# The second half of an out-product, its row norms and the MLP's first splits, moved into a table of ordered pieces

## The chip, the cores and the metric

One core of one Trainium2 chip. The time is device microseconds from launch to end; a run's profiled execution also gives a span, the time from its first to its last recorded instruction. TensorE, VectorE, ScalarE and GpSimd stand in the rows as PE, DVE, ACT and POOL, the queue that issues most of the loads as SP.

## The reference, cut to what matters

One encoder layer on x of 1024 tokens by 1024 features, float32. An mLSTM group (4 heads) and a differential attention group (4 heads) each give 512 features. Then:

```python
mixed = jnp.concatenate([mix_a, mix_b], axis=-1).astype(dt)
x = x + (mixed @ w_out[l]).astype(dt)
u = rms(x, norm2_g[l]).astype(dt) @ w_ff1[l]
u = jnp.square(jax.nn.relu(u))
x = x + (u @ w_ff2[l]).astype(dt)
```

`rms` divides each token by the root of the mean of its squares and multiplies by a gain. The change touches the line with `w_out`, the norm behind it and the preparation of `w_ff1`.

## The kernel before, in words

All activations lie transposed, 128 features on the partitions and tokens along the row, in two halves of 512 tokens. Every float32 product is made of three reduced-precision ones: each operand is split into a high part (ACT copies it into a rounded type) and a low part (DVE or POOL subtracts the high part from the raw value), and `mm3` issues high by high, high by low and low by high, each a matmul of 128x128 weights on a 128x512 tile. A split of a 128x1024 weight tile thus takes a load on SP into a raw buffer, a copy on ACT, a subtraction on DVE or POOL, and only then the low part's matmul can run.

**Attention.** 32 items (half, head, block of 128 queries). One item is: logits on PE and DVE, two exponentials on ACT, a weighted difference on DVE, transposes across on PE, copies on DVE and ACT, the product with the values on PE (`att_product`, line 981), a square on ACT with two small POOL operations (`att_square`, 988), a power on POOL (`att_root`, 996, through `rsqrt`, line 88), and the scaling `att_unit` on DVE (999). After every fourth item `att_turn`, `att_hi` and `att_lo` transpose the four blocks and split them into `mix`, the operand of the out-product.

**The table.** From line 1089 the order of each engine is written out by hand (`manual_schedule`): `when(t, f)` puts a piece on a heap with a due time in units of one attention item, the dictionary `A` holds the offsets, and the heap is emptied in order of time. Due times are no times on the chip: they fix only the order of the instructions on each engine and queue, and each instruction then waits for what it needs. The table holds the attention, the mLSTM group's output gates, and the out-product of the first half (`first_half`, line 1185, and `out_tile`, 1193): per output tile n = 0..7 two PE pieces of 12 matmuls, an addition of x on DVE, a square on ACT with a store, and a running sum of squares on DVE. Its weight splits come from `split_ahead` (1099), low part on POOL.

**Behind the table.** At line 1256 the hand-written order ends, and up to line 1359 the framework's planner orders the instructions by its own priorities: `load_mix(1)` (four loads of `mix` on POOL's queue), `out_product(1, ...)` (line 1029) with its splits through `split` (lines 131 to 134), the last `att_turn`, `att_hi` and `att_lo` (items 28 to 31), `row_norms(0)` (1074: eight small matmuls into `pr2`, an addition `rc` on DVE, the power on POOL, eight matmuls into `pb2`, a copy to `r2` on DVE), the normalisation of the first half (`normed`, 1325, two DVE instructions a call), its splits x1 and x2 (`cut`, 1298), and the first four splits of `w_ff1` (`w_a` with `raw_e`). In `out_product`, tile 0 and tile 1 begin before the last attention head is turned, with seven of eight feature blocks in the order (4, 5, 6, 0, 1, 2, 3, 7), and block 7 is added afterwards. The planner may place an instruction earlier than the program does, also between pieces of the table, or later.

**Behind that** the MLP has a hand-written order of its own (lines 1359 to 1787): twelve matmuls a step, `row_norms(1)` at its steps 0.95 and 1.95, then normalisation, sums and splits of the second half on DVE.

Of the kernel before, what the change touches and what calls it, by code (L numbers as in the profile page):

```python
# [16 lines left out]
P = 128  # L17
# [5 lines left out]
HB = 512  # L23
# [25 lines left out]
def hybrid_block_kernel(ctx: ExitStack, tc: tile.TileContext, xT, w_v, w_kg, w_c, w_va, w_qa, w_o, w_1, w_2, vec, rel, onehot, outT):  # L49
# [38 lines left out]
    def rsqrt(out, x, n):  # L88
        return nc.gpsimd.tensor_tensor(out, x, mhalf[:, 0:n], op=ALU.pow)
# [913 lines left out]
    def att_turn(items, V):  # L1003

        h, half = items[0].h, items[0].half
        po = psB.tile([P, HB], F32, tag="pav", name=f"pt{half}{h}")
        for it in items:
            nc.tensor.transpose(po[:, it.qi * P : (it.qi + 1) * P], it.on, ident)
        V["pr"] = po.rearrange("p (b t) -> p b t", t=P)[:, :, ::-1]

    def att_hi(it, V):
        V["mv"] = mv = mix[it.half][NH + it.h].rearrange("p i (b t) -> p i b t", t=P)
        nc.scalar.activation(mv[:, 0], V["pr"], AF.Copy, scale=dg[:, it.h : it.h + 1])
# [8 lines left out]
    def load_mix(half):  # L1022
        for h in range(NH):
            mix[half][h] = opool.tile([P, 2, HB], F32R, tag=f"mix{h}", name=f"mix{half}{h}")
            nc.gpsimd.dma_start(mix[half][h], mx_dram[h][half])

    r2, acc, rooted = {}, {}, {}

    def out_product(half, psum):
        sl = slice(half * HB, (half + 1) * HB)  # L1030
        acc[half] = opool.tile([P, HB], F32, tag="yacc", name=f"yacc{half}")
        order = (4, 5, 6, 0, 1, 2, 3, 7)
        ps, ws = {}, {}

        def load(n):
            if n < KT:
                ws[n] = split(opool, w_o[n], "wo", opool, 3, 2, nc.vector, f"wo{half}{n}")

        def part(n, first, end):
            if first == 0:  # L1040
                load(n)
                ps[n] = psum(n)
            (whi, wlo), p = ws[n], ps[n]
            for j in range(first, end):
                k = order[j]
                kt = slice(k * P, (k + 1) * P)
                mm3(p, whi[:, kt], wlo[:, kt], mix[half][k][:, 0], mix[half][k][:, 1], j == 0, j == KT - 1)


        part(0, 0, KT - 1)  # L1050
        part(1, 0, KT // 2)
        yield
        part(1, KT // 2, KT - 1)
        for n in range(KT):
            if n < 2:
                part(n, KT - 1, KT)
            else:
                part(n, 0, KT // 2)
                yield
                part(n, KT // 2, KT)  # L1060
            p = ps[n]
            yt = y[half][n]
            nc.sync.dma_start(yt, xT[n][:, sl])
            nc.vector.tensor_tensor(yt, p, yt, op=ALU.add)
            if n == 0:
                nc.scalar.activation(acc[half], yt, AF.Square)
            else:
                sq = opool.tile([P, HB], F32, tag="ysq", name=f"ysq{half}{n}", bufs=1)
                nc.scalar.activation(sq, yt, AF.Square)
                nc.vector.tensor_tensor(acc[half], acc[half], sq, op=ALU.add)  # L1070
            nc.scalar.dma_start(y_dram[half][n], yt)
            yield

    def row_norms(half):
        pc = psF.tile([P, HB], F32, tag="q2", name=f"pr2{half}")
        for t in range(4):
            nc.tensor.matmul(pc[:, t : t + 1], acc[half][:, t * P : (t + 1) * P], ones[:, 0:1], start=True, stop=True)
        rc = mpool2.tile([P, 4], F32, tag="rc", name=f"rc2{half}")
        nc.vector.tensor_scalar(rc, pc[:, 0:4], D * EPS, None, op0=ALU.add)
        rooted[half] = rsqrt(rc, rc, 4).ins  # L1080
        yield
        p = psF.tile([P, HB], F32, tag="q3", name=f"pb2{half}")
        for t in range(4):
            nc.tensor.matmul(p[:, t * P : (t + 1) * P], rc[:, t : t + 1].to_broadcast([P, P]), ident, start=True, stop=True)
        r2[half] = mpool2.tile([P, HB], F32, tag=("v", "w")[half], name=f"r2{half}")
        nc.vector.tensor_copy(r2[half], p)
# [3 lines left out]
    order.enter_context(tc.manual_schedule(engines={E.PE, E.DVE, E.Activation, E.Pool, E.SP}))  # L1090
    A = dict(
        G0=-0.05, G1=0.219, E0=0.984, E1=1.396, W=1.626, A0=2.667, A1=2.819, C0=2.714, C1=2.824, P=3.534, SQ=3.666,
        RS=3.676, ON=3.783, TU=4.131, TH=4.141, TL=4.151, LD=-2.901, LV=-1.095, PF=-4, PS=1.015, PE=0.388, PT=1.671,
        PB=1.957, PW=-3.566, PH=-2.613, PL=-1.973, PX=-0.258, SW=15.195, OF=18.423, OS=0.979, OE=0.323, OQ=0.587,
        OA=1.385, OW=-3.888, OH=-2.551, OL=-2.267,
    )
    clock[0] = -99.0

    def split_ahead(tiles, src, lo_eng, t, pre):

        T = {}

        def room():
            T[0] = tiles()
            nc.sync.dma_start(T[0][2][:, 0:1024], src)

        def hi():
            act(T[0][0][:, 0:1024], T[0][2][:, 0:1024], AF.Copy)

        def lo():  # L1110
            h, l, raw = T[0]
            lo_eng.tensor_tensor(l[:, 0:1024], raw[:, 0:1024], h[:, 0:1024].bitcast(F32), op=ALU.subtract)

        floor = A["SW"] + 0.01 if pre == "O" else -99.0
        when(max(t + A[pre + "W"], floor), room)
        when(max(t + A[pre + "H"], floor), hi)
        when(max(t + A[pre + "L"], floor), lo)
        return T
# [61 lines left out]
    def w_out(n):  # L1180
        raw = opool.tile([P, 1024], F32, tag="raw", name=f"raw_wo0{n}", bufs=2)
        hi = opool.tile([P, 1024], F32R, tag="woh", name=f"hi_wo0{n}", bufs=3)
        return hi, opool.tile([P, 1024], F32R, tag="wol", name=f"lo_wo0{n}", bufs=3), raw

    def first_half():

# [37 lines left out]
    def item_pieces(n, it):  # L1224
        def on(name, f, *args):
            when(n + A[name], f, it, *args)

        if n % 4 == 0:
            when(n + A["LD"] if n else -98.0, att_load, it)
            when(n + A["LV"] if n else -97.0, att_load_v, it)  # L1230
        for m in range(2):
            on(f"G{m}", att_logits, m)
            on(f"E{m}", att_exp, m)
            on(f"A{m}", att_across, m)
            on(f"C{m}", att_copy, m)
        on("W", att_weights)
        on("P", att_product)
        on("SQ", att_square)
        on("RS", att_root)
        on("ON", att_unit)  # L1240
        if n % 4 == 3 and n < 31:
            V = {}
            when(n + A["TU"], att_turn, items[n - 3 : n + 1], V)
            when(n + A["TH"], att_hi, it, V)
            when(n + A["TL"], att_lo, it, V)
# [3 lines left out]
    first_half()  # L1249
    for n, it in enumerate(items):  # L1250
        item_pieces(n, it)
    last = {}
    while table:
        t, _, f, args = heapq.heappop(table)
        f(*args)
    order.close()
    load_mix(1)

    def psum1(n):
        if n < 2:  # L1260
            return psB.tile([P, HB], F32, tag=("pw", "pa")[n], name=f"pw1{n}", bufs=n + 1)
        return psF.tile([P, HB], F32, tag=f"q{4 + n % 4}", name=f"pw1{n}")

    work = out_product(1, psum1)
    next(work)
    att_turn(items[28:32], last)
    att_hi(items[31], last)
    att_lo(items[31], last)
    bctx.close()


# [53 lines left out]
    def normed(l, j):  # L1325

        for n in (2 * j, 2 * j + 1):
            nc.vector.scalar_tensor_tensor(y[l][n], y[l][n], g2[:, n : n + 1], r2[l], op0=ALU.mult, op1=ALU.mult)
# [4 lines left out]
    def x_part(i, src, j):  # L1333
        return xf[i], src[j], (slice(None), slice(2 * j, 2 * j + 2))

    load_e(0)
    load_e(1)
    next(work)
    psctx.close()
    psF = ctx.enter_context(tc.tile_pool(reuse_waits="tile", name="psF", bufs=1, space=PSUM))  # L1340
    norms = row_norms(0)
    next(norms)
    for n, _ in enumerate(work):
        if n == 2:
            next(norms, None)
        if 3 <= n < 7:
            j = n - 3
            normed(0, j)
            cut(*x_part(1 + j // 2, block(j // 2, 0), j % 2))
        if 6 <= n < 10:  # L1350
            with tc.issue_after(rooted[0]):
                cut(w_a(n - 6), raw_e[n - 6])
            if n < 8:
                load_e(n - 4)
    cctx.close()
    x2pool = fctx.enter_context(tc.tile_pool(reuse_waits="tile", name="x2pool", bufs=1))
    xf |= {i: parts(x2pool, f"x{i}", [P, 4, HB]) for i in (3, 6, 5, 7, 4)}
# [22 lines left out]
    def psum(c, x):  # L1380
        q = 4 * (c % 2) + x
        if x == 0 and c < N_FIRST:
            q = (0, 1, 4, 5, 6, 7)[c]
        bank[c, x] = psF.tile([P, HB], F32, tag=f"q{q}", name=f"m{c}_{x}")
        return bank[c, x]
# [479 lines left out]
```

## Time and profile before

| | |
|---|---|
| median of 3 runs | 1292.5 us (1292.22 to 1293.47) |
| the profiled execution's own time | 1292.14 us |
| its span | 1290.4 us |
| PE busy | 1257.0 us (97%) |
| DVE, ACT, POOL busy | 860.0, 603.5, 272.6 us |
| mean granted TensorE clock | 0.993 of full speed |

Start times are microseconds from the span's start. In the timeline a row gives start, duration, engine, line, operation, output<-inputs and shapes; a bracket at the end is the idle time of the engine before that row and what released it. The rows of a matmul overlap: the distance between two starts is what one costs, the duration includes its latency. The attention's last items and the first half of the out-product end near 604 us, the second half ends where the first matmul of the MLP begins, and the MLP runs to the end.

### The profile page before, as it was taken

The page shows a single profiled execution, that of the slowest core. Times are in us where ns is not written, and L with a number is a line of the kernel's source. Part 1 is how long each engine was busy: PE and PEld are TensorE (multiplying, and loading weights), DVE is VectorE, ACT ScalarE, POOL GpSimd, SP SyncE. Part 2 cuts the span into 40 slices and gives each one's busy share as a digit, 9 for nine tenths or more (in the row PEclk, how much of TensorE's full clock was granted, in tenths as well). Part 3 has the DMA queues.
Part 4 walks back from the last instruction along what each step waited for, and adds up shares of the span by engine and source line. Part 5 has one row for each costly group of instructions (what it writes and reads, how often), then busy time and mean ns, then how long its engine had stood idle before and what let it go on. Part 6 is the DMA issues. An engine that isn't in the chain of part 4 may idle for free.

```text
span 1290.4 us, 17143 instructions
## 1 busy us (share of the span) xinstructions
PE 1257.0 (97%) x6443; PEld 1038.3 (80%) x6443; DVE 860.0 (67%) x1159; ACT 603.5 (47%) x1033; POOL 272.6 (21%) x273
## 2 busy tenths in 40 slices
PE   8999999999999989999999999999999999999998
PEld 6898678887878877888777788888887888888887
DVE  8635547886338888786748887666664675458754
ACT  5323336676535565563526554454444343333332
POOL 6623312554234344332000000000000000004001
PEclk9999999999999999999989999999999999999999
DMA  6415054544165475526524574454439946344732
GB/s 201 135 54 175 24 190 108 123 123 147 72 201 195 146 263 189 177 98 214 179 95 158 188 244 163 148 163 131 154 118 330 328 163 212 116 145 148 236 114 90
DMA packets 101459, 208.32 MB, mean 161 GB/s; under 512 B 8688, under 2 KB 21744, under 8 KB 101376
## 3 DMA queue, kind: packets, MB, share of 16 engines
q1 hardware_dynamic: 78368, 154.50, 37.6%
q10 hardware_dynamic: 15008, 31.50, 6.5%
q0 software_dynamic: 8000, 21.24, 5.0%
q8 instruction: 50, 0.82, 0.3%
q14 instruction: 33, 0.27, 0.1%
HBM read 148.90 MB, written 58.29 MB: 161 GB/s over the span
## 4 chain that ended last, share of the span: by engine, by line
PE 83%; DVE 8%; DMA 3%; issue 2%; ACT 2%; POOL 1%; SPq 0%; DVEq 0%; ACTq 0%; POOLq 0%
PE z L1707 8%; PE z L1705 8%; PE z L1706 8%; PE m L1376 7%; PE m L1377 7%; PE m L1378 7%; PE pav L986 4%; PE pl L945 3%; PE pv L235 3%; PE pw L158 2%; PE pa L972 2%; PE pw L160 2%; PE pw L159 2%; PE pj_c L158 2%; PE pj_c L159 2%
## 5 line engine op out<-in xcount | busy, mean ns | idle before, releaser
L1743 POOL TENSOR_TENSOR zx<-zx,res 128x512 f32<-128x512 f32 x4 | 8.7, 2180 | 503.8 <-DVE zx L1741 503.8
L1707 PE MATMUL z<-wbh,wa0l 128*128 128x512 f32 x224 | 87.4, 390 | 0.6 <-DVE wa0l L1296 0.6
L1705 PE MATMUL z<-wbh,wa0h 128*128 128x512 f32 x224 | 87.2, 389 | 0.0
L1706 PE MATMUL z<-wbl,wa0h 128*128 128x512 f32 x224 | 87.2, 389 | 0.0
L1706 PE MATMUL z<-wel,wa1h 128*128 128x512 f32 x224 | 87.1, 389 | 0.0
L1705 PE MATMUL z<-weh,wa1h 128*128 128x512 f32 x224 | 87.1, 389 | 0.0
L1707 PE MATMUL z<-weh,wa1l 128*128 128x512 f32 x224 | 87.1, 389 | 0.0
L950 DVE CUSTOM_DVE_ANT_0 l<-pl,toe 128x1024 f32<-128x1024 f32 x64 | 76.3, 1221 | 15.5 <-PE pl L945 14.4
L956 ACT ACTIVATE l<-l,sm 128x1024 f32<-128x1024 f32 x64 | 72.9, 1141 | 1.3 <-DVE sm L950 1.3
L1296 DVE TENSOR_TENSOR wel<-g,weh 128x1024 fp32r<-128x1024 f32 x28 | 35.2, 1258 | 56.5 <-ACT weh L1293 56.5
L1425 ACT ACTIVATE sq<-sq 128x512 f32<-128x512 f32 x48 | 30.3, 632 | 90.6 <-DVE sq L1464 69.0
L1296 DVE TENSOR_TENSOR wbl<-g,wbh 128x1024 fp32r<-128x1024 f32 x28 | 35.4, 1265 | 55.9 <-ACT wbh L1293 55.9
L1293 ACT ACTIVATE weh<-g 128x1024 fp32r<-128x1024 f32 x28 | 29.7, 1060 | 90.2 <-PE z L1707 53.4
L1293 ACT ACTIVATE wbh<-g 128x1024 fp32r<-128x1024 f32 x28 | 29.7, 1061 | 89.9 <-PE z L1707 52.6
L986 PEld LDWEIGHTS pav<-v,at 128*128 128x128 f32 x512 | 62.9, 195 | 9.3 <-DVE on L1001 4.6
L986 PE MATMUL pav<-v,at 128*128 128x128 f32 x512 | 64.4, 280 | 4.5 <-DVE on L1001 2.9
L160 PE MATMUL pw<-mix,lo_wo 128*128 128x512 f32 x128 | 51.5, 402 | 4.2 <-DVE lo_wo L134 4.2
L158 PE MATMUL pj_c<-hhi,hi_c 128*128 128x512 f32 x128 | 53.5, 418 | 0.0
L945 PE MATMUL pl<-kk,q 64*128 64x512 f32 x384 | 53.3, 408 | 0.0
L158 PE MATMUL pw<-mix,hi_wo 128*128 128x512 f32 x128 | 53.2, 415 | 0.0
L159 PE MATMUL pw<-mix,hi_wo 128*128 128x512 f32 x128 | 51.1, 399 | 0.0
L159 PE MATMUL pj_c<-hlo,hi_c 128*128 128x512 f32 x128 | 50.7, 396 | 0.0
(459 smaller groups left out, 3680.2 us busy)
## 6 DMA issues: line engine op xcount, KB each, us to landing
g<-g_dram SPq DMA_DIRECT2D x56, 512.0 KB, 4.1
g_dram<-gs SPq DMA_DIRECT2D x64, 256.0 KB, 4.3
g_dram<-sq ACTq DMA_DIRECT2D x42, 256.0 KB, 2.2
kk<-k_dram POOLq DMA_DIRECT2D x16, 512.0 KB, 5.6
raw_wo<-in_w_o_dram SPq DMA_DIRECT2D x16, 512.0 KB, 4.7
re<-in_w_dram SPq DMA_DIRECT2D x16, 512.0 KB, 4.4
ro<-in_w_dram SPq DMA_DIRECT2D x16, 512.0 KB, 3.7
zt<-in_w_dram SPq DMA_DIRECT2D x16, 512.0 KB, 4.1
```

Source lines behind the costliest of these rows:

```text
L158: nc.tensor.matmul(out, ahi, bhi, start=start, stop=False)
L159: nc.tensor.matmul(out, ahi, blo, start=False, stop=False)
L160: latest[0] = nc.tensor.matmul(out, alo, bhi, start=False, stop=stop).ins
L945: nc.tensor.matmul(it.pl[x][:, sl], hd.q[r, i, qi * P : (qi + 1) * P], hd.kk[r, j, sl], start=n == 0, stop=n == 2)
L950: nc.vector.tensor_tensor_reduce(lt, it.pl[m], hd.toe[:, off : off + S], 1.0, 3.0e38, ALU.add, ALU.min, it.sm[:, m : m + 1])
L986: nc.tensor.matmul(it.pav[:, 0:P], at, it.head.v[:, c], start=c == 0, stop=c == NC - 1)
L1376: nc.tensor.matmul(p, wh, xh, start=go, stop=False, skip_group_check=True)
L1377: nc.tensor.matmul(p, wh, xl, start=False, stop=False, skip_group_check=True)
L1378: nc.tensor.matmul(p, wl, xh, start=False, stop=stop and k == 3, skip_group_check=True)
L1705: nc.tensor.matmul(p, wh, gh, start=go, stop=False, skip_group_check=True)
L1706: nc.tensor.matmul(p, wh, gl, start=False, stop=False, skip_group_check=True)
L1707: nc.tensor.matmul(p, wl, gh, start=False, stop=end, skip_group_check=True)
```

## The change

Line 1256's end of the hand-written order goes away. Everything that the planner ordered is cut into pieces with due times in the same table, the part before `bctx.close()` (due before S2 = 35.3) and the part behind it. `out_product` is deleted. `load_mix(1)` is due at 33; the PE pieces of the second half begin at 34.3 and are 0.375 apart for 12 matmuls; `split_ahead` makes its splits (high on ACT 0.861 and low on DVE 0.4 ahead of a tile's first piece, never before the tile three back has been multiplied); `row_norms(0)` comes at 36.2 and 36.9, normalisation from 37.278, the splits of `w_ff1` from 37.523. The running sum of the second half has a buffer of its own (`yacc1`). `att_lo` of all turns moves from 4.151 to 4.177.

```diff
-    r2, acc, rooted = {}, {}, {}
-
-    def out_product(half, psum):
...
+    r2, acc = {}, {}
...
-        rooted[half] = rsqrt(rc, rc, 4).ins
+        rsqrt(rc, rc, 4)
...
-        RS=3.676, ON=3.783, TU=4.131, TH=4.141, TL=4.151, LD=-2.901, LV=-1.095, PF=-4, PS=1.015, PE=0.388, PT=1.671,
+        RS=3.676, ON=3.783, TU=4.131, TH=4.141, TL=4.177, LD=-2.901, LV=-1.095, PF=-4, PS=1.015, PE=0.388, PT=1.671,
...
+        OA=1.385, OW=-3.888, OH=-2.551, OL=-2.267, HF=34.3, HS=0.375, LM=33, HE=0.3, HQ=0.415, HA=0.425, HW=-1.4,
+        HH=-0.861, HL=-0.4, HX=-3.083, S2=35.3, N0=36.2, N1=36.9, XN=37.278, XD=0.78, XH=1.108, XL=1.118, WN=37.523,
+        WD=0.8, WL=0.227, RE=35.494,
...
-        if n % 4 == 3 and n < 31:
+        if n % 4 == 3:
...
-    while table:
-        t, _, f, args = heapq.heappop(table)
-        f(*args)
-    order.close()
-    load_mix(1)
+    def h_part(V, n, first, end):
+        if first == 0:
+            V[0] = psum1(n)
+        k_order = (4, 5, 6, 0, 1, 2, 3, 7)
+        hi, lo, _ = V["w"][0]
+        for j in range(first, end):
+            k = k_order[j]
+            kt = slice(k * P, (k + 1) * P)
+            mm3(V[0], hi[:, kt], lo[:, kt], mix[1][k][:, 0], mix[1][k][:, 1], j == 0, j == KT - 1)
+
+    def h_room(n):
+        nc.sync.dma_start(y[1][n], xT[n][:, HB:])
+
+    def h_add(V, n):
+        nc.vector.tensor_tensor(y[1][n], V[0], y[1][n], op=ALU.add)
...
-    work = out_product(1, psum1)
-    next(work)
-    att_turn(items[28:32], last)
-    att_hi(items[31], last)
-    att_lo(items[31], last)
+    when(A["LM"], load_mix, 1)
+    u = A["HS"]
+    parts_at = {0: ((0, 0, 7), (3.5, 7, 8)), 1: ((1.75, 0, 4), (2.75, 4, 7), (3.75, 7, 8))}
+    ends = {0: 3.75, 1: 4.0}
+    for n in range(2, KT):
+        parts_at[n] = ((2 * n, 0, 4), (2 * n + 1, 4, 8))
+        ends[n] = 2 * n + 2.0
+    def room_at(n):
+        return A["HF"] + u * ends[n - 3] + 0.01 if n > 2 else -99.0
+
+    for n in range(KT):
+        t = A["HF"] + u * parts_at[n][0][0]
+        V = {"w": split_ahead(lambda n=n: w_out(n, 1), w_o[n], nc.vector, t, "H", room_at(n))}
+        for p, first, end in parts_at[n]:
+            when(A["HF"] + u * p, h_part, V, n, first, end)
+        t = A["HF"] + u * ends[n]
+        when(max(t + A["HX"], A["S2"] + 0.02), h_room, n)
+        when(t + A["HE"], h_add, V, n)
+        when(t + A["HQ"], h_square, V, n)
+        when(t + A["HA"], h_sum, V, n)
...
+    run(A["S2"])
     bctx.close()
...
-    load_e(0)
-    load_e(1)
-    next(work)
...
-    next(norms)
-    for n, _ in enumerate(work):
...
+    when(A["N0"], next, norms)
+    when(A["N1"], next, norms, None)
+    for j in range(4):
+        t = A["XN"] + j * A["XD"]
+        when(t, normed, 0, j)
+        when(t + A["XH"], lambda a: cut_hi(*a), x_part(1 + j // 2, block(j // 2, 0), j % 2))
+        when(t + A["XL"], lambda a: cut_lo(*a), x_part(1 + j // 2, block(j // 2, 0), j % 2))
+        t = A["WN"] + j * A["WD"]
+        when(A["RE"] if j < 2 else t - 2 * A["WD"] + A["WL"] + 0.01, load_e, j)
+        when(t, lambda c: cut_hi(w_a(c), raw_e[c]), j)
+        when(t + A["WL"], lambda c: cut_lo(w_a(c), raw_e[c]), j)
+    run(1e9)
+    order.close()
```

`split_ahead` gets a `floor` for its three due times, `w_out` takes the half, `h_square` and `h_sum` do for the second half what `square` and `sum_up` of `out_tile` do for the first.

## Rows read from the trace of the kernel before

**Rows 1.** The page: its head, and busy time by engine.
```profile
span 1290.4 us, 17143 instructions
...
PE 1257.0 (97%) x6443; PEld 1038.3 (80%) x6443; DVE 860.0 (67%) x1159; ACT 603.5 (47%) x1033; POOL 272.6 (21%) x273
```

**Rows 2.** Windows: span, busy PE, PEld, DVE, ACT, POOL, then clock, DMA share, GB/s.
```profile
640.00:650.00 10.00, 5.82 (x22) 4.42 (x21) 9.31 (x12) 4.18 (x5) 0.00 (x0) 0.82 0.09 32
```

**Rows 3.** Timeline of PE: first matmuls of stretches, and those after idle time.
```profile
297.03 0.50 PE L159 MATMUL pva<-lo_va,hhi 128*128 128x512 f32 x1 [1.61 <-POOL lo_va L603]
...
587.20 0.66 PE L1008 MATMUL pt<-ident,on 128*128 128x128 f32 x4 [0.64 <-DVE on L1001]
...
603.93 0.48 PE L158 MATMUL pw<-mix,hi_wo 128*128 128x512 f32 x1
...
604.48 0.39 PE L160 MATMUL pw<-mix,lo_wo 128*128 128x512 f32 x1
...
625.49 1.16 PE L1084 MATMUL pb<-ident,rc 128*128 128x128 f32 x8 [1.43 <-POOL rc L89]
...
647.63 0.80 PE L160 MATMUL pw<-mix,lo_wo 128*128 128x512 f32 x1 [4.18 <-DVE lo_wo L134]
648.22 0.63 PE L158 MATMUL pw<-mix,hi_wo 128*128 128x512 f32 x1
...
653.28 0.39 PE L158 MATMUL pw<-mix,hi_wo 128*128 128x512 f32 x1
...
660.79 0.39 PE L1376 MATMUL m<-x1h,wa0h 128*128 128x512 f32 x1
...
711.05 0.61 PE L1376 MATMUL m<-x4h,wd0h 128*128 128x512 f32 x1 [2.40 <-DVE sq L1464]
711.46 0.63 PE L1377 MATMUL m<-x4l,wd0h 128*128 128x512 f32 x1
```

**Rows 4.** Timeline of DVE from 578 to 665 us, the pieces that matter.
```profile
578.52 3.17 DVE L134 TENSOR_TENSOR lo_wo<-raw_wo,hi_wo 128x1024 fp32r<-128x1024 f32 x1
...
602.41 1.23 DVE L134 TENSOR_TENSOR lo_wo<-raw_wo,hi_wo 128x1024 fp32r<-128x1024 f32 x1 [0.16 <-ACT hi_wo L133]
...
604.71 0.35 DVE L1001 TENSOR_SCALAR on<-pav,sm 128x128 f32<-128x128 f32 x1 [0.25 <-POOL sm L89]
604.98 0.68 DVE L1216 TENSOR_TENSOR yacc<-yacc,ysq 128x512 f32<-128x512 f32 x1
...
640.17 2.73 DVE L1328 SCALAR_TENSOR_TENSOR y<-y,cst,r 128x512 f32<-128x512 f32 x4
...
643.96 0.69 DVE L1064 TENSOR_TENSOR y<-pw,y 128x512 f32<-128x512 f32 x1
...
646.35 2.36 DVE L134 TENSOR_TENSOR lo_wo<-raw_wo,hi_wo 128x1024 fp32r<-128x1024 f32 x2
...
664.61 0.16 DVE L1079 TENSOR_SCALAR rc<-pr 128x4 f32<-128x4 f32 x1 [1.48 <-PE pr L1077]
```

**Rows 5.** Timeline of POOL from 593 to 605 us: powers, small products, loads it issues.
```profile
593.25 1.42 POOL L89 TENSOR_TENSOR sm<-sm,mhalf 128x1 f32<-128x1 f32 x1
...
595.10 1.70 POOL L1025 DMA_DIRECT2D mix<-mx_dram  x3
598.40 0.19 POOL L994 TENSOR_TENSOR sm<-sm 128x1 f32<-128x1 f32 x1 [1.60 <-ACT on L992]
...
603.85 0.19 POOL L994 TENSOR_TENSOR sm<-sm 128x1 f32<-128x1 f32 x1 [3.46 <-ACT on L992]
604.13 0.55 POOL L89 TENSOR_TENSOR sm<-sm,mhalf 128x1 f32<-128x1 f32 x1
```

**Rows 6.** DMA: `w_out` loads 575 to 670 us, line 1025's landing, throughput 606 to 612 us.
```profile
raw_wo<-in_w_o_dram SPq DMA_DIRECT2D x7, 512.0 KB, 3.9
...
DMA to landing us min/median/max: 3.9/6.6/11.3
...
DMA packets 762, 2.09 MB, mean 349 GB/s; under 512 B 84, under 2 KB 84, under 8 KB 760
```

More of the change, by code (lines that the diff above doesn't have):

```diff
@@ L1025, in load_mix @@
             nc.gpsimd.dma_start(mix[half][h], mx_dram[h][half])
-    r2, acc, rooted = {}, {}, {}
-    def out_product(half, psum):
[L1030 to L1072, printed above, removed]
+    r2, acc = {}, {}
     def row_norms(half):
@@ L1092, in hybrid_block_kernel, with split_ahead @@
         G0=-0.05, G1=0.219, E0=0.984, E1=1.396, W=1.626, A0=2.667, A1=2.819, C0=2.714, C1=2.824, P=3.534, SQ=3.666,
-        RS=3.676, ON=3.783, TU=4.131, TH=4.141, TL=4.151, LD=-2.901, LV=-1.095, PF=-4, PS=1.015, PE=0.388, PT=1.671,
+        RS=3.676, ON=3.783, TU=4.131, TH=4.141, TL=4.177, LD=-2.901, LV=-1.095, PF=-4, PS=1.015, PE=0.388, PT=1.671,
         PB=1.957, PW=-3.566, PH=-2.613, PL=-1.973, PX=-0.258, SW=15.195, OF=18.423, OS=0.979, OE=0.323, OQ=0.587,
-        OA=1.385, OW=-3.888, OH=-2.551, OL=-2.267,
+        OA=1.385, OW=-3.888, OH=-2.551, OL=-2.267, HF=34.3, HS=0.375, LM=33, HE=0.3, HQ=0.415, HA=0.425, HW=-1.4,
+        HH=-0.861, HL=-0.4, HX=-3.083, S2=35.3, N0=36.2, N1=36.9, XN=37.278, XD=0.78, XH=1.108, XL=1.118, WN=37.523,
+        WD=0.8, WL=0.227, RE=35.494,
     )
     clock[0] = -99.0
-    def split_ahead(tiles, src, lo_eng, t, pre):
+    def split_ahead(tiles, src, lo_eng, t, pre, floor=-99.0):
         T = {}
@@ L1112, in lo @@
             lo_eng.tensor_tensor(l[:, 0:1024], raw[:, 0:1024], h[:, 0:1024].bitcast(F32), op=ALU.subtract)
-        floor = A["SW"] + 0.01 if pre == "O" else -99.0
+        floor = max(floor, A["SW"] + 0.01 if pre in "OH" else -99.0)
         when(max(t + A[pre + "W"], floor), room)
@@ L1178, in hybrid_block_kernel, with w_out @@
     ypool = yq = y = cctx = opool = None
[L1180 to L1183, printed above, removed]
+    def w_out(n, half=0):
+        raw = opool.tile([P, 1024], F32, tag="raw", name=f"raw_wo{half}{n}", bufs=2)
+        hi = opool.tile([P, 1024], F32R, tag="woh", name=f"hi_wo{half}{n}", bufs=3)
+        return hi, opool.tile([P, 1024], F32R, tag="wol", name=f"lo_wo{half}{n}", bufs=3), raw
     def first_half():
@@ L1251, in hybrid_block_kernel, with h_square, h_sum @@
         item_pieces(n, it)
-    last = {}
-    while table:
-        t, _, f, args = heapq.heappop(table)
-        f(*args)
-    order.close()
-    load_mix(1)
+    def h_part(V, n, first, end):
[11 more added lines that the diff above has]
+        nc.vector.tensor_tensor(y[1][n], V[0], y[1][n], op=ALU.add)
+    def h_square(V, n):
+        if n == 0:
+            acc[1] = opool.tile([P, HB], F32, tag="yacc1", name="yacc1")
+        V["sq"] = acc[1] if n == 0 else opool.tile([P, HB], F32, tag="ysq", name=f"ysq1{n}", bufs=1)
+        nc.scalar.activation(V["sq"], y[1][n], AF.Square)
+        nc.scalar.dma_start(y_dram[1][n], y[1][n])
+    def h_sum(V, n):
+        if n > 0:
+            nc.vector.tensor_tensor(acc[1], acc[1], V["sq"], op=ALU.add)
     def psum1(n):
@@ L1262, in psum1, with run @@
         return psF.tile([P, HB], F32, tag=f"q{4 + n % 4}", name=f"pw1{n}")
-    work = out_product(1, psum1)
-    next(work)
-    att_turn(items[28:32], last)
-    att_hi(items[31], last)
-    att_lo(items[31], last)
+    when(A["LM"], load_mix, 1)
[17 more added lines that the diff above has]
+        when(t + A["HA"], h_sum, V, n)
+    def run(until):
+        while table and table[0][0] < until:
+            _, _, f, args = heapq.heappop(table)
+            f(*args)
+    run(A["S2"])
     bctx.close()
@@ L1341, in hybrid_block_kernel @@
     norms = row_norms(0)
-    next(norms)
-    for n, _ in enumerate(work):
[L1344 to L1354, printed above, removed]
+    when(A["N0"], next, norms)
[11 more added lines that the diff above has]
+    order.close()
     cctx.close()
```

## The prediction

> **What bounds the kernel now.** The page comes first: PE is busy 97% of the span [rows 1], so a reordering can only give back PE's idle time and what its clock loses. The windows around the change come next: from 640 to 650 us PE is busy 5.82 of 10 us at a granted clock of 0.82, while DVE is busy 9.31 [rows 2]. The timeline of PE then shows each wait in the stretch that is rewritten [rows 3]. The reader is to see four things. The turn of an attention head waits 0.64 us for a scaling on DVE (587.20). The second small product of the row norms waits 1.43 us for POOL's power (625.49). A low part of tile 6's weights comes 4.18 us late (647.63). And the matmuls behind that wait run at the lower of the clock's two levels, 1.2 GHz: 12 starts from 648.22 to 653.28 take 5.06 us, where 33 starts from 653.28 to 660.79 take 7.51, or 0.228 each at 2.4 GHz. The twelve lost 5.06 - 12 x 0.228 = 2.33, and the first, 0.59 against 0.228, another 0.36: together 2.69 us.
>
> The timeline of DVE says why. The first split of the second half, which the planner placed at 578.52, took 3.17 us inside the attention, where the same shape takes 1.23 at 602.41. The splits of tiles 6 and 7 were placed at 646.35, behind normalisation (640.17) and an addition (643.96) that PE did not need yet [rows 4].
>
> **The change, part by part.** The number of matmuls, splits, additions, loads and stores stays the same; what changes is order and one more small buffer. I give times on the clock of the kernel before.
>
> 1. *The first split leaves the attention.* From 578.52, 3.17 us of DVE go, and with them the lateness that PE saw at 587.20: gain 0.64. From there to 603.93 PE had no further wait that this could shorten, so I count nothing more. Two later splits also leave; they cost PE nothing before.
>
> 2. *The first split's new place.* Its low part is now due at 33.9, behind the scaling of item 30 (33.783), and DVE's queue is in order. That scaling waits for POOL: it started at 604.71 and the next DVE instruction at 604.98 [rows 4]. The split then ends at 604.98 + 1.23 = 606.21. PE reaches tile 0 at 603.93, and the third matmul, the first with a low part, would start at 604.48 [rows 3]. New wait: 606.21 - 604.48 = 1.73 us. Queued behind it on PE are 18 more matmuls and item 31's product, and behind that its square, power, scaling and turn, all of which PE itself reaches later. The low part of tile 1 follows behind the running sum of tile 7 of the first half (0.68): 606.21 + 0.68 + 1.23 = 608.1, against 19 matmuls of tile 0 and item 31's product still to run. Hidden.
>
> 3. *Does the clock fall at that wait?* Not shown for 1.73 us. A single wait of 1.61 us (297.03) was followed by a matmul of 0.50, no half-speed run, as was the one of 1.43; the one of 2.40 at 711.05 was followed by matmuls of 0.63 [rows 3]. The bounds are 0 and 2.69 us; 1.73 lies next to 1.61, so I take 0.
>
> 4. *The four loads of `mix` on POOL's queue.* They were issued from 595.10, at 1.70 / 3 = 0.57 each; now they follow item 29's power and stand ahead of item 30's two small operations. Item 29's first operation is at 598.40; with the gaps of item 30's (603.85, 604.13, 0.55 long) its power ends at 599.23, the four issues at 601.5, 2 us before POOL is wanted at 603.85 [rows 5]. Nothing waits. Their landing took 3.9 to 11.3 us [rows 6]. PE needs the first after nine matmuls of tile 0, at 606.21 + 7 x 0.228 = 607.8; issued by 599.8, it has 8.0 us. At the median of 6.6 this costs nothing; at 11.3 from the issue's start at 599.23 it is 2.7 us late. I take 0.
>
> 5. *SP's queue.* The split of tile 2 reloads a buffer that the split of tile 0 frees, so SP stops until 606.2. Behind it stand five loads of x, two of `w_ff1` and tile 3's weights. With tile 2's own load that is 2 x 0.5 + 5 x 0.25 + 2 x 0.5 = 3.25 MiB, 9.8 us at 349 GB/s [rows 6], so tile 3 has landed by 616. It is wanted when tile 0 has got its last block and frees the high part, not before 606.21 + 43 x 0.228 = 616.0 plus item 31's product and turn. Tile 2's landing (3.9 us) is over by 610.5. The later weight loads follow a split made some 10 us before their own use. Zero; if that cover went, tile 3's split (ACT's copy and DVE's 1.23 us) would show.
>
> 6. *The row norms.* The two small products now have 12 matmuls between them, 2.7 us, for the chain DVE, POOL, PE. In the second norm the addition `rc` came at 664.61, with the MLP's first twelve matmuls just done at 660.79 + 12 x 0.228 = 663.5 as the product began, and the same spacing gave PE no wait behind it. DVE now stands still for `rc` about 4 us while PE multiplies tile 2; ahead of it is tile 3's split, so PE is not held. Gain 1.43.
>
> 7. *The later splits.* DVE's order now has the split of tile n + 2 soon behind the addition of tile n. A tile is 24 matmuls, 5.46 us. The heaviest period on DVE holds three splits, two normalisations, a sum and an addition: 3 x 1.23 + 2.73 / 2 + 0.68 + 0.69 = 6.43 us [rows 4]. There are two such periods, so additions slip by at most 1 and 2 us. Tile 6's split ends 0.69 + 2 x 1.23 = 3.15 after tile 4 does, 2.3 us before it is wanted; tile 7's ends about 1 + 0.69 + 1.23 = 2.9 after tile 5, 2.5 us before. Gain 4.18, and with the wait the 2.69 of the clock.
>
> 8. *Behind the out-product.* DVE's last piece is now one split of x2, due behind the last sum, but its high part waits on ACT behind the last square. It ends about when `rc` could start, 3.82 us after the first MLP matmul (664.61 against 660.79). Cost 0; the bounds are 0 and 1.23. The MLP's own waits (2.40 at 711.05 and smaller ones) hang on that DVE chain and move with it. Moving `att_lo` by 0.026 passes no other piece of DVE: nothing.
>
> Sum: -0.64 + 1.73 - 1.43 - 4.18 - 2.69 = -7.21 us. Against the profiled execution, 1292.14, that is 1284.9. The median of the runs is 0.36 above that execution, so I forecast **1285.3 us**. A measurement of this kernel can tell 0.2%, 2.6 us, from no change.
>
> **Rivals.**
>
> *The new wait grows.* The clock falls at the wait of point 2: 1285.3 + 2.69 = 1288.0. For it: 1.73 lies above the longest wait without a fall; against it: PE is busy without a gap for 16 us ahead. Still faster.
>
> *POOL's queue holds item 30.* A power beside a DVE instruction took 1.42 us instead of 0.55 [rows 5]. If each of the four issues is stretched by the same 0.87, they end 4 x 0.87 - 2.05 = 1.4 us too late for item 30, the wait becomes 3.1 and the clock falls: 1285.3 + 1.4 + 2.69 = 1289.4. Against it: the three issues that ran beside DVE's work at 595.10 took 0.57 each, and DVE has only short work on PSUM then. The Trainium skill, "SBUF — State Buffer", section "SBUF: two separate sides", speaks against this part of the change: VectorE and GpSimd share a port pair as an exclusive lock, and loads issued from GpSimd can be starved of descriptors while VectorE holds it. Its example, in the section "A bandwidth-pool intuition that's wrong (but worth ruling out)", stretches one such load from about 620 to 3100 ns; by that estimate four take 12.4 us, item 30 is 8.1 late, and the sum gives 1296.1, slower than before. The issues of 0.57 us beside busy DVE don't bear that out here.
>
> *DVE becomes the bound: slower.* The place is the split of tiles 6 and 7 in DVE's queue, behind splits of x1 and of `w_ff1`. If two tiles wait as tile 6 did before, each costs 4.18 + 2.69 = 6.87, and the result is 1285.3 + 13.7 = 1299.0. It decides once DVE needs more than 5.46 + 2.3 = 7.8 us for a tile's period; 6.43 is known. Splits as long as the 3.17 at 578.52 would do it, but POOL's work that stood beside that one is over by then.
>
> *Given back in the MLP.* DVE bounds PE up to 711.05. If its work there does not start earlier by what PE gains, the time stays between 1290 and 1295. Against it: `rc` starts the chain, and it follows the out-product's last sum.
>
> *The change doesn't do what it says.* Due times fix order, not time; if PE's waits hung on loads and not on order, they would stay, and so would 1292.5. The row at 647.63 names the DVE split, not a load.
>
> **Chances.** The forecast 0.55, the clock's fall at the new wait 0.18, POOL's queue by rows 0.04, no new wait at all (1283.6) 0.04; given back 0.08, no effect 0.03; DVE-bound 0.06, POOL's queue by the page's rule 0.02. Faster: 0.55 + 0.18 + 0.04 + 0.04 = 0.81. Same: 0.08 + 0.03 = 0.11. Slower: 0.06 + 0.02 = 0.08. The range goes down to no new wait and none at 711.05, 1283.6 - 2.4 = 1281.2, and up to the clock's fall with the slow landing of point 4, 1288.0 + 2.7 = 1290.7.
>
> **What would show it.** Right: no turn of a head waiting near 587; one wait of 1.5 to 2 us at the third matmul of tile 0, released by the split on DVE; full clock from there to the MLP; no wait at the second small product; the first MLP matmul near 653.6. Wrong: matmuls of 0.63 us behind the new wait, a wait on `lo_wo` at tiles 5 to 7, loads of `mix` landing after 607, or a longer distance from the first MLP matmul to the x4 wait than 711.05 - 660.79 = 50.3 us.

## The result, and the profile after

| | before | after |
|---|---|---|
| median of 4 runs each, same chip | 1292.36 us | 1286.29 us (1284.2 to 1287.63) |
| ratio, 95% interval | | 0.995 (0.9933 to 0.9968) |
| the profiled execution's own time | 1292.14 us | 1285.70 us |
| mean granted clock | 0.993 | 0.996 |

The changed kernel is 6.1 us faster by the medians, 6.4 by the profiled executions; 7.2 were forecast. The page's head and busy times, beside [rows 1]:

```profile
span 1283.9 us, 17139 instructions
...
PE 1254.5 (98%) x6443; PEld 1036.1 (81%) x6443; DVE 857.2 (67%) x1159; ACT 603.0 (47%) x1033; POOL 269.9 (21%) x273
```

The work is the same and PE's share is higher: what went is waiting. In [rows 2] PE was busy 5.82 of 10 us at a clock of 0.82. Windows of the same stretch after, with the columns of [rows 2]:

```profile
640.00:650.00 10.00, 10.00 (x46) 8.29 (x45) 10.00 (x13) 5.75 (x7) 0.00 (x0) 1.00 0.42 130
```

PE no longer pauses there, and neither does DVE: the two now run abreast. PE's timeline, beside [rows 3]:

```profile
586.00 0.66 PE L1008 MATMUL pt<-ident,on 128*128 128x128 f32 x4
...
602.74 0.48 PE L158 MATMUL pw<-mix,hi_wo 128*128 128x512 f32 x1
...
605.07 0.50 PE L160 MATMUL pw<-mix,lo_wo 128*128 128x512 f32 x1 [1.62 <-DVE lo_wo L1069]
605.40 0.40 PE L158 MATMUL pw<-mix,hi_wo 128*128 128x512 f32 x1
...
627.04 1.05 PE L1039 MATMUL pb<-ident,rc 128*128 128x128 f32 x8
...
652.45 0.39 PE L1374 MATMUL m<-x1h,wa0h 128*128 128x512 f32 x1
...
696.79 0.50 PE L1375 MATMUL m<-x7l,weh 128*128 128x512 f32 x1 [1.24 <-DVE x7l L1297]
...
703.41 0.47 PE L1374 MATMUL m<-x4h,wd0h 128*128 128x512 f32 x1 [2.40 <-DVE sq L1462]
```

The turn at 586.00 and the second small product at 627.04 have no bracket any more. The new wait, 1.62 us, stands at the third matmul of tile 0, and the matmul behind it takes 0.40: full clock. From there to the MLP PE waits for nothing. The last two rows are the MLP's, and the first of them has grown: the same matmul, 704.43 before, waited 0.54 us there.

**Where the 6.5 us of span came from.** Three stretches, each from the start of one row to that of another, and their sum:

| stretch | before | after | difference |
|---|---|---|---|
| start to the out-product's tile 0 | 603.93 | 602.74 | -1.19 |
| tile 0 to the MLP's first matmul | 56.86 | 49.71 | -7.15 |
| MLP to the end of the span | 629.6 | 631.45 | +1.84 |
| span | 1290.4 | 1283.9 | -6.5 |

The second row is the change's own, and I measure every experiment by it. Of the first, 0.64 is the turn's wait; 0.48 was there already at 541 us, where the same matmul of the logits starts at 541.04 before and at 540.56 after, and 0.51 already at 297 us (the row at 297.03 in [rows 3] starts at 296.52 after), far ahead of anything that the change touches.

### The profile page after: what moved, and what is told of

It is laid out like the page before. It is cut to its first block, busy times and chain, and to the rows that moved or that the text cites. A ratio compares the mean times of both kernels' runs of the same rounds, so it can differ in the third digit from the quotient of the medians.

```text
span 1283.9 us, 17139 instructions
## 1 busy us (share of the span) xinstructions
PE 1254.5 (98%) x6443; PEld 1036.1 (81%) x6443; DVE 857.2 (67%) x1159; ACT 603.0 (47%) x1033; POOL 269.9 (21%) x273
## 4 chain that ended last, share of the span: by engine, by line
PE 85%; DVE 6%; DMA 3%; ACT 2%; issue 2%; POOL 1%; SPq 0%; ACTq 0%; DVEq 0%; POOLq 0%
PE z L1705 8%; PE z L1703 8%; PE z L1704 8%; PE m L1374 7%; PE m L1375 7%; PE m L1376 7%; PE pav L986 4%; PE pl L945 3%; PE pv L235 3%; PE pw L158 2%; PE pw L160 2%; PE pw L159 2%; PE pa L972 2%; PE pj_c L158 2%; PE pj_c L159 2%
## 5 line engine op out<-in xcount | busy, mean ns | idle before, releaser
L158 PE MATMUL pw<-mix,hi_wo 128*128 128x512 f32 x128 | 52.3, 408 | 0.0
L160 PE MATMUL pw<-mix,lo_wo 128*128 128x512 f32 x128 | 50.3, 393 | 1.6 <-DVE lo_wo L1069 1.6
L160 PE MATMUL pj_c<-hhi,lo_c 128*128 128x512 f32 x128 | 50.5, 394 | 0.0
```

## The experiments

Each is the changed kernel with one edit; where a diff has `lo_at`, `split_ahead` takes the due time of a tile's low part from that dictionary. "The stretch" is the distance from tile 0's first matmul to the MLP's first; one profiled execution each. The medians are of all executions of a run. They were taken in three groups: changed_again, first_split_early, late_splits_back and wait_three; late_split_tile4, norms_adjacent, wait_two and split_in_attention; first_split_again and ro_load_later. The kernel before had 1292.4, 1292.1 and 1292.27 us beside them; the groups ran on different chips.

**changed_again.** No edit.

> The changed kernel a second time, nothing edited. Its first four runs lay 3.4 us apart (1284.2 to 1287.6), those of the kernel before 1.6. Theory: the order of the instructions is fixed, so the part up to the MLP repeats (third matmul of tile 0 waits 1.6 us, first MLP matmul 49.7 us after tile 0 begins), and what varies is DMA landing in the MLP: the x4 wait comes 50.3 to 51.5 us after the first MLP matmul. Rival: the clock sometimes falls at the new wait of tile 0, then 2.7 us are lost there in some runs and matmuls of 0.63 us stand behind the wait. Median expected 1286 (both).

1285.49 us (1283.96 to 1288.41, 6 runs), ratio 0.9947 (0.9935 to 0.996). The stretch is 604.27 to 653.95 = 49.68 us, 0.03 from the first time; the wait at tile 0 is 1.61 us and the clock stays. The MLP to the end took 1283.1 - 653.95 = 629.15 us, 0.5 less than before the change, not 1.84 more, and the x4 wait came 49.88 us behind the MLP's first matmul, sooner than the 50.3 to 51.5 expected. So it is not given back there in every execution. PE's timeline of this run in the MLP:

```profile
703.83 0.47 PE L1374 MATMUL m<-x4h,wd0h 128*128 128x512 f32 x1 [2.49 <-DVE sq L1462]
704.14 0.39 PE L1375 MATMUL m<-x4l,wd0h 128*128 128x512 f32 x1
```

No half-speed run followed the wait of 2.49, where in the first execution eight matmuls of 0.59 to 0.63 followed one of 2.40. The stretch is steady to 0.03 us and the rest of the program is not: that is why the median of ten runs (these and the first four), 1285.9, says less than a row.

**late_splits_back.** The low parts of tiles 6 and 7, and tile 6's matmuls, go to the end of the table, as the planner had them.

```diff
+    lo_at = {6: 39.23, 7: 39.231}
-            when(A["HF"] + u * p, h_part, V, n, first, end)
+            when({(6, 0): 39.24, (6, 4): 39.25}.get((n, first), A["HF"] + u * p), h_part, V, n, first, end)
```

> The low parts of tiles 6 and 7 are due at 39.23, behind the second split of x1 and a sum, as the planner had them behind a split of x2; the two PE pieces of tile 6 keep their order. Theory: DVE does an addition, a split and a sum first (0.69 + 1.22 + 0.68) and then the split, so the third matmul of tile 6 waits 3.3 to 3.8 us, the clock falls behind it and costs 2.7 more, and the time is 6.0 to 6.5 us above the changed kernel's, 1292 to 1293: the two largest terms of the gain are undone alone. Rival (the gain came from the shared reordering, or DVE is the bound anyhow): under 2 us above the changed kernel's.

1291.75 us (1287.95 to 1292.46, 10 runs): the size came, by another way. PE's timeline:

```profile
642.50 0.39 PE L1374 MATMUL m<-x1h,wa0h 128*128 128x512 f32 x1
...
645.88 0.50 PE L160 MATMUL pw<-mix,lo_wo 128*128 128x512 f32 x1 [0.32 <-DVE lo_wo L1069]
...
658.94 1.76 PE L1032 MATMUL pr<-ones,yacc 128*128 128x1 f32 x8 [2.32 <-DVE yacc L1236]
660.56 0.77 PE L1374 MATMUL m<-x1h,wa1h 128*128 128x512 f32 x1
661.13 0.63 PE L1375 MATMUL m<-x1l,wa1h 128*128 128x512 f32 x1
```

The MLP's first twelve matmuls now stand behind tile 6's first two and ahead of its third: at the border of the two hand-written orders they slipped in front of pieces due so late. They covered the wait for the split (0.32 us left), but the second row norm, behind them, then waited 2.32 us for a running sum that was late, and the clock fell behind it. A time that agrees is no proof of the mechanism, so the test was made again in the middle of the table.

**late_split_tile4.** The low part of tile 4 and its matmuls are due behind the first split of `w_ff1`.

```diff
+    lo_at = {4: 37.76}
-            when(A["HF"] + u * p, h_part, V, n, first, end)
+            when({(4, 0): 37.77, (4, 4): 37.78}.get((n, first), A["HF"] + u * p), h_part, V, n, first, end)
```

> The low part of tile 4's weights is due at 37.76, behind the addition of tile 3, the split of tile 5, a sum and a split of w_ff1, and the two PE pieces of tile 4 at 37.77 and 37.78; the order on PE is the same, and nothing of the MLP is ready that could fill the gap. Theory (each of the late splits of the kernel before cost its wait and the clock): the split ends near 635.6 on the changed kernel's clock where the third matmul of tile 4 would start at 631.4, so 4.2 us of wait and 2.7 of the lower clock, 6.9 together, near 1292.4. Rival 1 (no fall of the clock in the middle of dense matmuls): 4.2 only, near 1289.7. Rival 2 (DVE bounds this stretch anyhow): under 2.

1292.32 us (1290.46 to 1293.4, 10 runs), ratio 0.9998 (0.9989 to 1.0008): this one edit undoes the whole gain. DVE's timeline, then PE's:

```profile
634.58 1.22 DVE L1297 TENSOR_TENSOR wa0l<-re,wa0h 128x1024 fp32r<-128x1024 f32 x1
635.71 1.22 DVE L1069 TENSOR_TENSOR lo_wo<-raw_wo,hi_wo 128x1024 fp32r<-128x1024 f32 x1
```

```profile
636.98 0.80 PE L160 MATMUL pw<-mix,lo_wo 128*128 128x512 f32 x1 [4.34 <-DVE lo_wo L1069]
637.58 0.63 PE L158 MATMUL pw<-mix,hi_wo 128*128 128x512 f32 x1
```

The wait of 4.18 us is back as 4.34, with the lower clock behind it, at another tile. In the profile the stretch is 659.76 - 604.08 = 55.68, 6.0 longer. What is over the wait, 1.65, is less than the 2.69 of before: full clock is back after seven matmuls here (at 640.02), after thirteen there [rows 3].

**norms_adjacent.** The second small product of the first norm is due right behind the first.

```diff
-        ... N0=36.2, N1=36.9, ...
+        ... N0=36.2, N1=36.21, ...
```

> The second small product of the row norms is due at 36.21, directly behind the first, so that no matmuls cover the chain DVE, POOL, PE. Theory: the chain is 2.7 us from the start of the first product (the addition starts 1.06 behind it, the power 0.24 later and takes 1.0 to 1.9), the first product itself 0.8, so PE waits 1.5 to 2.3 us at the second, without a fall of the clock; 1.5 to 2.3 us more than the changed kernel, near 1287.4. Rival (the earlier copy of r2 lets DVE run ahead and gives it back): no more than 0.5 us.

1287.47 us (1286.38 to 1288.3, 4 runs), 2.0 over changed_again. PE's timeline:

```profile
626.76 1.16 PE L1039 MATMUL pb<-ident,rc 128*128 128x128 f32 x8 [1.35 <-POOL rc L89]
```

The stretch is 654.99 - 603.82 = 51.17, 1.49 longer than changed_again's; the wait is just under the 1.5 to 2.3 expected. The term of 1.43 stands.

**first_split_early.** The low part of tile 0 is due ahead of item 30's scaling.

```diff
+    lo_at = {0: 33.70}
```

> The low part of tile 0's weights is due at 33.70, ahead of item 31's copy and item 30's scaling, instead of 33.90. Theory (the wait is only DVE's queue order): no wait at the third matmul of tile 0, the first MLP matmul 1.6 us earlier relative to the attention, the time 1.6 us under the changed kernel's, near 1284.6. Rival 1 (the wait moves: item 31's copy or item 30's scaling becomes late, or the loads of mix have not landed): PE waits 1 us or more at another place before tile 1, gain under 0.6. Rival 2 (given back in the MLP): the first MLP matmul is earlier by 1.6 but the time is not.

1282.48 us (1280.86 to 1283.46, 5 runs), ratio 0.9922 (0.991 to 0.9933). Tile 0 has no wait, and the stretch is 651.22 - 603.40 = 47.82, 1.86 shorter than changed_again's: the wait and the start behind it, which takes 0.33 instead of 0.23. It beats both kernels. By median it is 3.0 under changed_again where 1.6 was expected; 1.1 of it lie outside the stretch.

**wait_two and wait_three.** The other way: the low part of tile 0 behind the running sum, and behind tile 1's split as well, with the first piece of tile 0 moved to 34.51 to keep its place on PE.

```diff
+    lo_at = {0: 34.5}               # wait_two
+    lo_at = {1: 34.495, 0: 34.5}    # wait_three
```

> The low part of tile 0 is due behind the running sum alone, so its wait grows from 1.6 to 2.2 us, between the 1.62 without a fall of the clock and the 3.62 with one. Theory A (a single wait on a busy PE of this length leaves the clock alone): 0.6 us more than the changed kernel, near 1286.1, matmuls of 0.39 behind the wait. Theory B (it falls): 0.6 + 2.7 = 3.3 us more, near 1288.8, a dozen of 0.63.

> The low part of tile 0 is due behind the running sum and the low part of tile 1, so that its wait grows from 1.6 to about 3.6 us; the order on PE is the same. Theory (a wait of this length on a busy PE lets the clock fall, as after 4.18 us before): 12 or so matmuls of 0.63 us behind the wait and 2.0 + 2.7 = 4.7 us more than the changed kernel, near 1291. Rival (the clock does not fall there): 2.0 us more, near 1288.3.

1287.32 us (1284.7 to 1288.34) and 1288.65 us (1286.14 to 1290.29), 4 runs each. PE's timelines of the two:

```profile
606.97 0.80 PE L160 MATMUL pw<-mix,lo_wo 128*128 128x512 f32 x1 [2.21 <-DVE lo_wo L1069]
607.56 0.63 PE L158 MATMUL pw<-mix,hi_wo 128*128 128x512 f32 x1
...
610.12 0.44 PE L158 MATMUL pw<-mix,hi_wo 128*128 128x512 f32 x1
610.40 0.39 PE L159 MATMUL pw<-mix,hi_wo 128*128 128x512 f32 x1
```

```profile
608.01 0.80 PE L160 MATMUL pw<-mix,lo_wo 128*128 128x512 f32 x1 [3.62 <-DVE lo_wo L1069]
608.60 0.63 PE L158 MATMUL pw<-mix,hi_wo 128*128 128x512 f32 x1
```

Behind 2.21 us the clock is at its lower level for seven matmuls: the eight starts from 606.97 to 610.40 take 3.43 us where 8 x 0.228 = 1.82 would do. The stretch is 51.83, 2.15 longer, of which 0.6 is the wait. For wait_three it is 54.20, 4.5 longer: 2.0 of wait and 2.5 of clock. These are one execution each. The medians say less: wait_two is 1.8 over changed_again's, between the 0.6 and the 3.3 of the two theories, and wait_three 3.2 over, nearer to the 2.0 without a fall than to the 4.7 with one; its profiled execution, 1290.29, was the slowest of its four. Whether the clock fell in the others too isn't shown. In these two executions it did fall, in the first at a wait only 0.6 us longer than the changed kernel's: the rival "the new wait grows" was a real danger.

**split_in_attention.** The load, copy and low part of tile 0 go back into the attention.

```diff
+    lo_at = {0: 29.87}
-        when(max(t + A[pre + "W"], floor), room)
-        when(max(t + A[pre + "H"], floor), hi)
+        when(max(t + A[pre + "W"], floor) if lo_at != 29.87 else 29.55, room)
+        when(max(t + A[pre + "H"], floor) if lo_at != 29.87 else 29.6, hi)
```

> The split of tile 0 goes back to where the planner had it, into item 30's DVE work: load, copy and low part due at 29.55, 29.60 and 29.87, beside POOL's low part of the first half's tile 7. Theory (term 1 of the sum and the new wait of term 2 are the same split at two places): the DVE instruction takes about 3.2 us instead of 1.22, the turn of the head near 587 waits 0.6 us, tile 0 does not wait; 1.6 - 0.6 = 1.0 us under the changed kernel, near 1284.5. Rival (its stretch by POOL was chance): it takes 1.2 us, no wait at the turn, 1.6 us under.

1286.48 us (1283.48 to 1288.74, 5 runs), 1.0 above changed_again's median, where a gain of 1.0 was expected. PE's timeline, then POOL's and DVE's:

```profile
588.14 0.65 PE L1008 MATMUL pt<-ident,on 128*128 128x128 f32 x4 [0.64 <-DVE on L1001]
...
611.66 0.50 PE L158 MATMUL pw<-mix,hi_wo 128*128 128x512 f32 x1 [2.29 <-DMA mix<-mx_dram]
```

```profile
579.12 2.43 POOL L1069 TENSOR_TENSOR lo_wo<-raw_wo,hi_wo 128x1024 fp32r<-128x1024 f32 x1
```

```profile
579.47 3.17 DVE L1069 TENSOR_TENSOR lo_wo<-raw_wo,hi_wo 128x1024 fp32r<-128x1024 f32 x1
```

The split of 3.17 us and the turn's wait of 0.64 came back to the hundredth [rows 3, 4], and tile 0's wait for the split went. But a new one came, on `mix`, at the nineteenth matmul of tile 0, the first that needs the last of the four loads. First SP's and POOL's issues in the timeline, then the landing of the four loads, in this run and in the first execution of the changed kernel:

```profile
594.11 5.33 SPq L1313 DMA_DIRECT2D re<-in_w_dram  x2
```

```profile
600.11 2.23 POOL L1025 DMA_DIRECT2D mix<-mx_dram  x4
```

```profile
DMA to landing us min/median/max: 4.7/6.6/9.8
```

```profile
DMA to landing us min/median/max: 3.9/5.8/7.8
```

The last load landed 2.0 us later behind its issue, and PE, which no longer waited at the third matmul, wanted it 1.8 us sooner. Why it landed later stays open. SP's queue, no longer stopped by tile 0's buffer, had sent the loads of `w_ff1` ahead of it, and moved 0.48 MB from 600 to 602 us while POOL's moved 0.01; but in the changed kernel POOL's queue, with next to nothing else moving, got only 0.08 in its first two microseconds. In the four that follow it moved 1.17 MB here and 1.48 there, and SP's moved 0.02, so bytes of SP's queue in that time are not the reason.

The stretch is 50.53, 0.85 longer: -1.86 for the wait that went, +2.29 for the one that came; the 0.4 that is left wasn't followed further. The turn's 0.64 lies ahead of the stretch.

**first_split_again and ro_load_later.** The first is first_split_early once more; the second adds one edit in the MLP, where in the first execution of the changed kernel a sum on DVE waited 1.08 us:

```profile
694.91 0.69 DVE L1453 TENSOR_TENSOR v<-m,x_b 128x512 f32<-128x512 f32 x1 [1.08 <-DMA ro<-in_w_dram]
```

The bracket names a load of `ro`, which `v` doesn't read; before the change the same row (702.55, a wait of 0.38) named the store of `v_s`, whose buffer `v` takes. I took that store, slowed by the loads, for the cause. Its row in the DMA view, of the first execution and then of first_split_again, where `v` did not wait (the last number is the time to landing in us):

```profile
g_dram<-v_s ACTq DMA_DIRECT2D x1, 256.0 KB, 6.0
```

```profile
g_dram<-v_s ACTq DMA_DIRECT2D x1, 256.0 KB, 4.6
```

```diff
-    when(12.5, load_o, 2)
+    when(14.1, load_o, 2)
```

> The kernel of first_split_early once more, unedited, as the comparison for ro_load_later on the same chip. Theory (no wait at tile 0, the MLP's x4 wait left at 2.4 to 2.5 us): 1282.5 us by median again, within 1.5. Rival (its 3.0 us under changed_again was half luck of the MLP's waits): 1284 us, which is changed_again's median less the 1.6 us of the wait at tile 0.

> first_split_early with the third pair of row loads of the MLP (ro) issued at 14.1 instead of 12.5 in the MLP's table, so that the store of v_s, whose buffer the next sum v takes, is not shared with two 512 KB loads. Theory (the MLP gave back 0.7 us because that store landed 0.7 us later beside those loads): the wait of v on DVE goes, x4's wait on PE comes some 0.7 us earlier and shrinks, and the kernel is 0.5 to 1 us faster than first_split_again. Rival (PE waits at x4 for the DVE chain whatever the store does, or the later load is itself waited for): the wait at x4 stays at 2.4 us or moves to v's wait on ro, and the time is first_split_again's or up to 2 us longer.

1284.15 us (1281.81 to 1285.2) and 1283.13 us (1282.5 to 1285.27), 5 runs each. No difference can be told: the sum waited in neither. The first is at the rival's 1284 and just outside the theory's 1282.5 give or take 1.5, so a part of the 3.0 of first_split_early was chance. The sum's row in first_split_again, with the load where it was, and the x4 wait of both:

```profile
692.23 0.68 DVE L1453 TENSOR_TENSOR v<-m,x_b 128x512 f32<-128x512 f32 x1
```

```profile
700.72 0.47 PE L1374 MATMUL m<-x4h,wd0h 128*128 128x512 f32 x1 [2.39 <-DVE sq L1462]
```

```profile
704.05 0.77 PE L1374 MATMUL m<-x4h,wd0h 128*128 128x512 f32 x1 [2.40 <-DVE sq L1462]
```

So `v` waits in some executions and not in others, with the loads in the same place. All twelve traces of this case point to the store as what it waits for: in the eight in which `v` waits, the store took 5.3 to 6.1 us to land and `v` began 0.2 to 0.3 behind it; in the four in which it does not, 4.2 to 4.7. That the loads slow the store is not shown: it took 4.6 with them where they were and 4.7 with `ro` later. And x4's wait stays at 2.4 us either way: what `v`'s wait costs is that x4 comes 0.7 to 1.2 us later, not that its wait grows. Of the 3.5 us by which the spans of the two profiled executions differ, 3.27 lie ahead of tile 0 (603.10 against 606.37), in code that the edit doesn't touch. The stretch was 47.82 and 47.89. Over its ten runs the kernel of first_split_early has a median of 1283.3, 2.6 under the changed kernel's ten, of which 1.9 is in the stretch.

## Why the prediction was right, point by point

1. *The first split leaves the attention: shown.* The turn waits for nothing at 586.00, and split_in_attention brought the 0.64 back. The Trainium skill, "SBUF — State Buffer", section "SBUF: two separate sides", says that GpSimd and a VectorE instruction with two inputs in SBUF exclude each other at a shared port pair, and that the later one waits for the whole of the earlier. The trace of split_in_attention agrees with it for the 3.17 us: POOL began a split of 2.43 us at 579.12, DVE's began at 579.47, so 2.08 of waiting and 1.22 of work would make 3.3.
2. *The new wait: right.* The split follows the scaling directly, as worked out:

```profile
603.53 0.35 DVE L1001 TENSOR_SCALAR on<-pav,sm 128x128 f32<-128x128 f32 x1 [0.26 <-POOL sm L89]
603.80 1.22 DVE L1069 TENSOR_TENSOR lo_wo<-raw_wo,hi_wo 128x1024 fp32r<-128x1024 f32 x1
```

The third matmul of tile 0 starts at 605.07 instead of 602.74 + 0.55 = 603.29, 1.78 us late for a forecast of 1.73. The bracket says 1.62, since it counts only the time after the matmul before has ended.

3. *No fall of the clock there: right,* in all five traces that have the wait (1.61 or 1.62 us in each, the matmul behind it 0.39 or 0.40). The neighbour on which it rested, 1.61 us [rows 3], was the right one; at 2.21 us in the same place the clock did fall.
4. *The loads of `mix`: right at nothing, in part by luck.* On POOL's queue the margin was as forecast. POOL's timeline:

```profile
597.97 2.23 POOL L1025 DMA_DIRECT2D mix<-mx_dram  x4
...
602.66 0.19 POOL L994 TENSOR_TENSOR sm<-sm 128x1 f32<-128x1 f32 x1 [2.11 <-ACT on L992]
```

Four issues in 2.23 us are 0.56 each, and POOL then stood idle for 2.11 (forecast: 2.05). The estimate by the Trainium skill, "SBUF — State Buffer", section "A bandwidth-pool intuition that's wrong (but worth ruling out)", 12.4 us for the four, is not borne out in this place; but DVE ran only one scaling of 0.35 us in that time and then stood idle for 1.95, so this is no test of the rule. The landing cost nothing, but not for the reason given. The 3.9 to 11.3 us that point 4 took from [rows 6] are of eight loads, four of them those of the first half; the four that the change moves had landed in 3.9 to 5.9 before, and after the change in 3.9 to 7.8. The last of them landed near 599.7 + 7.8 = 607.5, so the sign "landing after 607" came, without a cost: PE wants that block at 608.83. The new wait at tile 0 gave 1.78 us of that: without it PE would have wanted the block at 607.05, before it landed. In split_in_attention, where that wait is gone, PE waits 2.29 us; in first_split_early the four landed in 6.8 us at most, and it does not.

5. *SP's queue: right.* ACT waits 2 us for tile 3's load, and PE doesn't notice:

```profile
617.40 1.06 ACT L148 ACTIVATE hi_wo<-raw_wo 128x1024 fp32r<-128x1024 f32 x1 [2.03 <-DMA raw_wo<-in_w_o_dram]
```

The load landed near 617.4; 616 was worked out.

6. *The row norms: right,* 1.43 forecast, 1.49 by norms_adjacent. DVE stands still for `rc` as said, 4.4 us for "about 4":

```profile
624.36 0.16 DVE L1034 TENSOR_SCALAR rc<-pr 128x4 f32<-128x4 f32 x1 [4.40 <-PE pr L1032]
```

7. *The later splits: right.* Tiles 6 and 7 are split at 638.07 and 642.87, and no tile waits:

```profile
638.07 1.22 DVE L1069 TENSOR_TENSOR lo_wo<-raw_wo,hi_wo 128x1024 fp32r<-128x1024 f32 x1
...
642.87 1.21 DVE L1069 TENSOR_TENSOR lo_wo<-raw_wo,hi_wo 128x1024 fp32r<-128x1024 f32 x1
```

Putting one split behind a normalisation and a split of `w_ff1` (late_split_tile4) costs the 4.18 and, in the profiled execution, a part of the 2.69.

8. *Behind the out-product: the step that failed, at no cost.* The forecast had the last split of x2 ahead of `rc`; it ran behind it, beside POOL's power, which took 1.92 us where it took 1.01 before:

```profile
656.27 0.16 DVE L1034 TENSOR_SCALAR rc<-pr 128x4 f32<-128x4 f32 x1 [1.48 <-PE pr L1032]
656.35 1.22 DVE L1297 TENSOR_TENSOR x2l<-y,x2h 128x1024 fp32r<-128x1024 f32 x1
```

```profile
656.51 1.92 POOL L89 TENSOR_TENSOR rc<-rc,mhalf 128x4 f32<-128x4 f32 x1 [30.51 <-DVE rc L1034]
```

`rc` starts 3.82 us after the MLP's first matmul, exactly as before. The power ended at 658.43, and the MLP's matmuls cover it: the product that needs it starts at 658.83 without a wait.

**The sum.** For tile 0 to the MLP the forecast was +1.73 - 1.43 - 4.18 - 2.69 = -6.57; it measured -7.15. The 0.6 between come mostly from two things. The terms 1.43 and 4.18 were taken from brackets, and a bracket is less than the delay of a start: 623.67 to 625.49 and 643.06 to 647.63 are 1.82 and 4.57, which less one matmul's 0.228 are 1.59 and 4.34. That is 0.3 for the two. And a term was missed: item 31's product used to cut into tile 0 behind four matmuls (0.41 + 1.80 + 0.32 between starts from 604.71 to 607.24) and now runs between whole blocks (1.70 + 0.31 from 609.51), 0.3 less once a plain matmul's 0.228 is taken from the first. With the turn's 0.64 the change gives 7.8 us where it acts. The medians show 6.1 and 6.9. What lies between must be in the stretches it doesn't touch: over the eleven traces of the changed kernel and of its variants tile 0 began between 602.74 and 606.37, 603.96 on average, and the MLP to the end took 629.1 to 631.45, 630.04 on average (all but late_splits_back, whose border moved). The kernel before has one trace, with 603.93 and 629.6. So the 0.64 of the turn can't be seen at tile 0's start against this spread, though the wait itself is gone; whether the two stretches are on average longer than before stays open. "Given back in the MLP" was ruled out as a rule by changed_again; in the first execution it cost 1.84 us, 0.7 of it ahead of x4's wait: the sign "more than 50.3 us to x4" came there (703.41 - 652.45 = 50.96) and not in changed_again (49.88).

## What to carry to other kernels

When PE is 97% busy, look for the few waits in which the *order* of another engine's queue is at fault, and price each with the clock behind it: one late split, with the clock that fell behind it, was worth nearly all that this change gained. A bracket is the engine's idle time; the delay of the start is what a removed wait gives back. A wait that can't be avoided is best kept as short as those which the trace shows without a fall behind them, and often it can be avoided by one more move in the same queue, as in first_split_early. Before a wait is removed, ask what it was covering: the one at tile 0 also gave the last load of `mix` 1.8 us more to land.

## What the runs showed of the hardware

- The granted clock after a single wait is not told by the wait's length alone in these rows: 1.61, 1.62 no fall; 2.21 a fall of seven matmuls; 2.29 (split_in_attention) none; 2.32 (late_splits_back) a fall; 2.38 to 2.49 at x4 a fall in some executions and none in others; 3.62, 4.18 and 4.34 a fall. What decides between 2.2 and 2.5 was not tried.
- Four loads of 512 KB issued on POOL's queue moved little in the two microseconds from the first issue, whether another queue was moving (0.01 MB in split_in_attention, beside 0.48 on SP's) or not (0.08 in the changed kernel); in the next four they moved 1.17 and 1.48.
- A subtraction of 128x1024 on DVE that began 0.35 us behind the same on POOL took 3.17 us, where it takes 1.22 alone (split_in_attention).
- A due time past the end of one hand-written order let the next order's matmuls slip in front (late_splits_back).
